# A pair's keys get their norm first, activation sums go one in two steps, and residual reloads wait for a split

## The chip, the cores and the metric

The kernel runs on one core of one Trainium2 chip. The metric is the device time of one execution in microseconds (us); less is better. The core has five engines with a queue of instructions each: TensorE (PE in the profile, its weight loads PEld) multiplies matrices, VectorE (DVE) and ScalarE (ACT) work elementwise, GpSimd (POOL) does some elementwise work and issues transfers, SyncE (SP) issues transfers. Each queue runs in its own order; semaphores hold an instruction until what it reads is there.

## The reference

One decoder layer on a sequence of 512 tokens, width 2048, in float32. Cut to what matters here:

```python
h = rms_norm(x, attn_norm)
proj = h @ w_in
qf, kf, vf, ff, qn, kc, vc, ks, vs, kw, vw, gt = split(proj)
qf = rms_norm(qf, fox_q_norm)          # 8 "fox" heads of 128
kf = rms_norm(kf, fox_k_norm)
s = einsum(qf, kf) * scale + cum[q] - cum[k]
o_fox = masked_softmax(s) @ vf
...
o_nsa = gate0 * o_c + gate1 * o_s + gate2 * o_w
x = x + concat(o_fox, o_nsa) @ w_out
h = rms_norm(x, ffn_norm)
x = x + (silu(h @ w_gate) * (h @ w_up)) @ w_down
```

`cum` is a running sum of log gates, so the fox heads have a bias for every pair of query and key. The other eight heads (compressed, selected and window branches, merged by gates) are computed earlier and are touched by the change only in passing.

## The kernel before

**Products.** Each float32 operand is split in a high and a low part of a shorter type. ACT writes the high part (`act(..., AF.Copy)`, L95), DVE the rest by a subtraction (`tt`, L92). A product is three matmuls, high by high, high by low and low by high (`mm3`, L259 to L261; L1057 and L1379 are the same in other loops). So each tile of weights passes SP (load), ACT (high part), DVE (low part) and PE, which may start a tile when the high part is there and needs the low part two matmuls later. `ws_*` are the loaded weights, `wp_*` their parts.

**Seven products for eight.** Most projections work by a scheme that replaces eight products of half matrices by seven, with sums of weights and sums of activations. The sums of activations are the "forms": `forms_45`, `forms_6` and `forms_3` make them on DVE (L976, L977, L984, L985, L994) and ACT (L991), a few instructions at each step, into `f4_u`, `f5_u`, `f6_u` for u from 0 to 7. They are first needed in the pair phase below.

**Stages.** The stretch that the change touches runs from about 390 to 840 us. First come the last single projections, `stagger(kf(1), qf(1), vf(2))`: the keys and queries of head 1 and the values of head 2. Beside them, woven in, run head 0's attention, and a generator `extra` with the forms: `among(main, extra, start, every)` takes a step of `extra` behind every so many steps of `main`. In this stage `extra` has 30 steps: five each of `forms_45` for u of 5, 6 and 7, and three each of `forms_6` for u of 0 to 4. What is left of it when `main` ends is run by `run(extra)`.

Then comes the pair phase. `seven` computes for a pair of outputs the seven products; `pair(h)` gives one head's keys and queries this way, `vpair(h)` the values of two heads. After its products a pair normalizes both outputs: their squares (`squares`), the sums over a head by a matmul with ones (`ss_k*`, L1104; `ss_q*`, L431), reciprocal square roots, and splits into parts. For the keys that gives `kf*`; for the query a split tile `qq`, and the four small instructions L443 to L446 on DVE that make `qs_q*`, the factors by which scores are scaled. This second part of `pair` runs beside the next pair's products.

Beside the products run the attentions of the heads 1 to 7 (`fox`, stepped by `attend`). `SPANS` gives for each head the ticks between which its 17 steps are spread; a tick is a step of the loop over pairs. A head multiplies scores in four blocks of query rows (`s_f*3` with 512 columns, then 384, 256 and 256), for which GpSimd makes bias tiles `nbf` from the factors (L847, L848); DVE adds the bias and finds the maxima (L602), ACT takes exponentials (L608) and scales (L617, `p_f`), PE transposes (`pT_f`, L633), and the transposed probabilities are multiplied by the values (`of`).

The output projection (from about 660 us) uses the seven products again. Its residual sums x1 are written to `x1d` in DRAM by GpSimd's queue (L1268). `form_again(pair)` reloads the tiles `pair` and `pair + 8` as `x1r` (L1285, GpSimd's queue as well, 256 KB each), from which the second half of the layer gets its raw forms. Its weights are loaded and split by `parts_apart`.

**Order.** In the attention stages a scheduler decides the order in each engine's queue, from dependencies and the order of the code; a step moved in the code moves rows on all engines. In the output projection and behind it the order is that of the code. `highs` is a list of instructions that wrote high parts; its last one serves as a time mark for transfers that shall not start earlier.

Of the kernel before, what the change touches and what calls it, by code (L numbers as in the profile page):

```python
# [9 lines left out]
F32 = mybir.dt.float32  # L10
# [7 lines left out]
P = 128  # L18
# [65 lines left out]
def hybrid_layer(ctx: ExitStack, tc: tile.TileContext, xT, vec, ffb, wfg, wfirst, win, cmpw, wout, wos, wgu, wdn, out):  # L84
# [123 lines left out]
    def split2(dst, src, scale=None):  # L208

        if scale is None:  # L210
            h = act(dst[0], src, AF.Copy)
            tt(dst[1], src, dst[0].bitcast(F32), op=OP.subtract)
        else:
            h = act(dst[0], src, AF.Copy, scale=scale)
            nc.vector.scalar_tensor_tensor(dst[1], src, scale, dst[0].bitcast(F32), op0=OP.mult, op1=OP.subtract)
        return h
# [153 lines left out]
    def gain(i):  # L370
        return gains[:, i:i + 1]
# [42 lines left out]
    def squares(name, z):  # L414

        sq = ftile(f"sq_{name}")
        sb = ap_.tile([P, T], F32, tag="sb", name=f"sb_{name}")
        nc.scalar.activation(sq[half], z[half], AF.Square)
        nc.scalar.activation(sb[half], z[second_half], AF.Square)
        nc.vector.tensor_tensor(sq[half], sq[half], sb[half], op=OP.add)  # L420
        return sq

    def square_sums(name, sq, tag, bufs=1):

        fr = ap_.tile([P, T], FR, tag="fr", name=f"fr_{name}")
        o = ps.tile([P, NB, 2], F32, tag=tag, name=f"ss_{name}", bufs=bufs)
        split2([fr[half], fr[second_half]], sq[half])
        if bufs > 1:
            yield
        for i in range(NB):  # L430
            nc.tensor.matmul(o[:, i], fr[:, i * P:(i + 1) * P], ones[:, :2], start=(i == 0), stop=(i == NB - 1), skip_group_check=True)  # L431
        return o
# [16 lines left out]
    def place():  # L449
        r = qq[:, turns[0] % 2]  # L450
        turns[0] += 1
        return [r[:, p] for p in range(2)]
# [630 lines left out]
    def pair(h):  # L1083

        k, q = [f"{m}f{h}" for m in "kq"]
        t, z = yield from seven(("p", h), (k, q))
        yield POST
        assert h - 2 in scored
        r = place()
        split2(r, z, gain(V_FQ))  # L1090
        sq = squares(q, z)
        yield
        oq = square_sums(q, sq, "t", 2)
        next(oq)
        yield
        sq = squares(k, t)
        yield
        oq = yield from oq
        fr = ap_.tile([P, T], FR, tag="fr", name=f"fr_{k}")
        split2([fr[half], fr[second_half]], sq[half])  # L1100
        yield
        yield
        ok = ps.tile([P, T], F32, tag="t", name=f"ss_{k}", bufs=2)
        nc.tensor.matmul(ok, ones, fr, start=True, stop=True)  # L1104
        yield
        live[q] = r, *factors(q, oq)
        y = ftile(f"y_{k}")
        rsqrt(y, ok, float(HD), ftile(f"tmp_{k}"), False)
        nc.vector.scalar_tensor_tensor(t, t, gain(V_FK), y, op0=OP.mult, op1=OP.mult)
        r = ap_.tile([P, KV], FR, tag="kv", name=k, bufs=5)[:, 64:64 + 2 * T].rearrange("p (s t) -> p s t", s=2)  # L1110
        first_keys[k] = r[:, :, :P]
        r = [r[:, p] for p in range(2)]
        split2(r, t)
        live[k] = r
        yield

    def vpair(h):
# [13 lines left out]
    def among(main, extra, start, every):  # L1131
        for i, _ in enumerate(main):
            yield
            if i >= start and (i - start) % every == 0:
                next(extra, None)
# [3 lines left out]
            next(steps, None)  # L1139
            yield  # L1140

    SPANS = {1: (0, 45), 2: (45, 73), 3: (73, 101), 4: (101, 157), 5: (157, 185), 6: (185, 213), 7: (213, 241)}
    STEPS = 17
    tick = [0]
    heads = {h: fox(h) for h in SPANS}
# [35 lines left out]
    live["x6"] = only.enter_context(tc.tile_pool(name="x6", bufs=1, side="right"))  # L1181
    paced[0] = 4
    extra = chain(*[forms_45(u, True) for u in range(5, HALF)], *[forms_6(u) for u in early6])
    weave(among(stagger(kf(1), qf(1), vf(2)), extra, 0, 1), fox(0), 4 * NK, FS, 18)
    run(extra)
    extra = chain(*[forms_3(u) for u in range(HALF)])
    assert nproj[0] == FIRST7
# [93 lines left out]
    def form_again(pair):  # L1281

        ts = [ftile(f"x1r_{n}") for n in (pair, pair + HALF)]
        for i, t in enumerate(ts):
            nc.gpsimd.dma_start(t, x1d[pair + HALF * i])  # L1285
        yield
        for i, t in enumerate(ts):
            raw_forms(pair + HALF * i, t)
        raw = live["raw"]
        form_sums(raw)  # L1290
        dst = forms[pair].rearrange("p s f t -> p s (f t)")
        src = raw[:, 0:7].rearrange("p f t -> p (f t)")
        if pair < 6:
            act(dst[:, 0], src, AF.Copy)
        yield
        if pair == 6:
            act(dst[:, 0], src, AF.Copy)
        tt(dst[:, 1], src, dst[:, 0].bitcast(F32), op=OP.subtract)
        yield
# [42 lines left out]
    def parts_apart(src, name, off):  # L1342
        st = ws_tile(f"{name}")
        load(st, src)
        wp = parts_tile(f"wp_{name}")
        wp = [cut(wp, at + off, HALF * P) for at in (0, HALF * P)]
        act(wp[0], st, AF.Copy)
        yield
        tt(wp[1], st, wp[0].bitcast(F32), op=OP.subtract)
        yield  # L1350
        return wp
# [693 lines left out]
```

## Time and profile before

| | |
|---|---|
| runs, median of 3 | 2089.14 us (2088.11 to 2091.69) |
| the profiled execution | 2089.46 us |
| its span | 2087.8 us |
| PE busy | 2063.7 us |
| DVE, ACT, POOL busy | 1803.2, 1070.4, 323.9 us |
| mean granted clock of PE | 0.998 of full speed |
| DMA packets | 424.22 MB |

The span runs from the first to the last instruction in the profile. A row of a timeline gives start, duration, engine, line, operation and the tiles with buffer numbers left out, and in brackets how long the engine idled before it and what released it. Durations of matmuls overlap, since they are pipelined: what one costs PE is the distance from its start to the next one's. PE's waits are few: the page's busy share is 99%.

### The profile page before, as it was taken

The numbers are of one execution on the slowest core, as the hardware profiler recorded it, in microseconds if no ns is written. First come the engines' busy times: TensorE is split into PE (matmuls) and PEld (weight loads), VectorE is DVE, ScalarE is ACT, GpSimd is POOL, SyncE is SP. The second block draws the span as 40 slices with busy tenths as digits, with TensorE's granted clock in tenths as the row PEclk, the third lists the DMA queues.
The fourth block names the chain that finished last, engine by engine and source line by source line (L and its number), as shares of the span: only waits on it lengthen the run. The fifth ranks groups of instructions, "written<-read, shape, count | busy, mean of one in ns | idle before, by whom it ended". The sixth has DMA issues, their size and how long they took to land.

```text
span 2087.8 us, 40036 instructions
## 1 busy us (share of the span) xinstructions
PE 2063.7 (99%) x16189; PEld 1976.5 (95%) x16189; DVE 1803.2 (86%) x2744; ACT 1070.4 (51%) x1408; POOL 323.9 (16%) x489
## 2 busy tenths in 40 slices
PE   9999999899999999999999999999999999999999
PEld 8888989799998988999999999999999999999999
DVE  6688779878777877999999999999999987889998
ACT  6555556457676555443343344433433455565554
POOL 1032232422121011111111111111111000000000
PEclk9999999999999999999999999999999999999999
DMA  5685776867775575676767777777777797579865
GB/s 211 208 183 164 178 173 180 196 172 209 219 187 187 189 238 184 169 209 185 194 191 189 203 183 184 210 182 198 188 190 203 241 327 258 155 237 329 298 177 149
DMA packets 142153, 424.22 MB, mean 203 GB/s; under 512 B 17608, under 2 KB 17608, under 8 KB 141968
## 3 DMA queue, kind: packets, MB, share of 16 engines
q1 hardware_dynamic: 91168, 289.21, 41.3%
q0 software_dynamic: 44176, 106.19, 26.6%
q10 hardware_dynamic: 6624, 26.27, 3.3%
q8 instruction: 126, 2.06, 0.4%
q14 instruction: 59, 0.48, 0.1%
HBM read 389.34 MB, written 124.53 MB: 246 GB/s over the span
## 4 chain that ended last, share of the span: by engine, by line
PE 87%; DVE 6%; ACT 4%; issue 2%; DMA 1%; POOL 0%; ACTq 0%; SPq 0%; POOLq 0%; DVEq 0%
PE q L1790 39%; PE pd L1929 13%; PE pd L1934 7%; PE ps_kf L1057 3%; PE ps_vs L540 2%; PE ps_vf L540 2%; PE po L261 2%; PE po L260 2%; PE po L259 2%; PE po L1379 1%; PE ps_qn L259 1%; PE ps_qn L261 1%; PE ps_qn L260 1%; PE ps_first L261 1%; PE ps_first L259 1%
## 5 line engine op out<-in xcount | busy, mean ns | idle before, releaser
L95 ACT ACTIVATE bigm<-r 128x1792 fp32r<-128x1792 f32 x174 | 298.3, 1714 | 462.6 <-PE q L1790 315.6
L92 DVE TENSOR_TENSOR bigm<-r,bigm 128x1792 fp32r<-128x1792 f32 x174 | 351.3, 2019 | 10.2 <-ACT bigm L95 9.7
L92 DVE TENSOR_TENSOR r<-r 128x512 f32<-128x512 f32 x522 | 267.1, 512 | 30.1 <-DMA r<-wgu 18.0
L141 POOL DMA_DIRECT2D wsum<-wdn x176 | 120.1, 689 | 702.2 <-ACT bigm L95 609.4
L1790 PE MATMUL q<-bigm 128*128 128x256 f32 x1848 | 217.5, 276 | 0.2
L1790 PE MATMUL q<-formy,bigm 128*128 128x256 f32 x1848 | 216.9, 276 | 0.0
L1790 PE MATMUL q<-forma,bigm 128*128 128x256 f32 x1848 | 216.8, 276 | 0.0
L1790 PE MATMUL q<-formx,bigm 128*128 128x256 f32 x1848 | 216.8, 276 | 0.0
L1790 PEld LDWEIGHTS q<-bigm 128*128 128x128 f32 x1848 | 213.3, 188 | 0.6 <-DVE bigm L92 0.3
L1790 PEld LDWEIGHTS q<-forma,bigm 128*128 128x128 f32 x1848 | 213.0, 188 | 0.1
L1790 PEld LDWEIGHTS q<-formy,bigm 128*128 128x128 f32 x1848 | 213.0, 188 | 0.1
L1790 PEld LDWEIGHTS q<-formx,bigm 128*128 128x128 f32 x1848 | 212.9, 188 | 0.0
L1929 PE MATMUL pd<-bigm 128*128 128x256 f32 x1200 | 146.9, 276 | 0.0
L1929 PEld LDWEIGHTS pd<-bigm 128*128 128x128 f32 x1200 | 141.0, 188 | 0.0
L92 DVE TENSOR_TENSOR bigm<-wd,bigm 128x1024 fp32r<-128x1024 f32 (+1 forms) x62 | 107.7, 1738 | 13.3 <-ACT bigm L95 13.0
L95 ACT ACTIVATE bigm<-rawm 128x768 fp32r<-128x768 f32 (+2 forms) x72 | 66.0, 927 | 96.8 <-PE pd L1934 62.2
L95 ACT ACTIVATE bigm<-wd 128x1024 fp32r<-128x1024 f32 (+1 forms) x62 | 91.1, 1469 | 12.1 <-DVE wd L92 6.1
L92 DVE TENSOR_TENSOR bigm<-rawm,bigm 128x768 fp32r<-128x768 f32 (+2 forms) x72 | 75.5, 1057 | 23.1 <-ACT bigm L95 22.3
L1934 PE MATMUL pd<-bigm 128*128 128x256 f32 x600 | 80.7, 276 | 0.0
L141 POOL DMA_DIRECT2D fsump<-win x72 | 48.5, 742 | 203.3 <-ACT wp_qn L95 46.8
L1057 PE MATMUL ps_kf<-bigm,wp_kf 128*128 128x256 f32 x576 | 77.0, 282 | 1.0 <-ACT wp_kf L95 0.9
L1057 PEld LDWEIGHTS ps_kf<-bigm,wp_kf 128*128 128x128 f32 x576 | 71.6, 188 | 3.0 <-ACT wp_kf L95 1.8
(592 smaller groups left out, 4342.0 us busy)
## 6 DMA issues: line engine op xcount, KB each, us to landing
r<-wgu SPq DMA_DIRECT2D x174, 512.0 KB, 4.4
wsum<-wdn POOLq DMA_DIRECT2D x176, 256.0 KB, 5.0
rawm<-ad SPq DMA_DIRECT2D x44, 512.0 KB, 6.8
wd<-wdn SPq DMA_DIRECT2D x40, 512.0 KB, 6.0
wd<-wsum SPq DMA_DIRECT2D x40, 512.0 KB, 7.1
ad<-cb ACTq DMA_DIRECT2D x22, 896.0 KB, 6.5
fsump<-win POOLq DMA_DIRECT2D x72, 256.0 KB, 6.2
rawm<-ad SPq DMA_DIRECT2D x44, 384.0 KB, 3.6
```

Source lines behind the costliest of these rows:

```text
L92: return pin(nc.vector.tensor_tensor(*args, op=op))
L95: return pin(nc.scalar.activation(*args, **kw))
L141: d = nc.gpsimd.dma_start(step[0], step[1], **step[2])
L259: nc.tensor.matmul(o, lh, rh, start=start, stop=False)
L260: nc.tensor.matmul(o, lh, rl, start=False, stop=False)
L261: nc.tensor.matmul(o, ll, rh, start=False, stop=stop)
L540: nc.tensor.matmul(z[2 * b + t][:, :cols[n]], x[:, xp, at], wp[n][kk], start=(c == 0 and kk == 0 and n == 0 and (t == 0 or gcols is not No ...
L1057: nc.tensor.matmul(z, w[wp][:, u * P:(u + 1) * P], form(f, u)[xp], start=(fresh and m == 0), stop=(m == len(todo) - 1), skip_group_check=True)
L1379: nc.tensor.matmul(q[b][:, h * 256:(h + 1) * 256], w[wp][:, u * P:(u + 1) * P], a[xp], start=(h == 0 and u == 0 and wp == 0 and xp == 0), ...
L1790: nc.tensor.matmul(o, w[wp][:, fb, cs], a[:, xp, fa], start=(k == 0 and h == 0 and wp == 0 and xp == 0), stop=(g == NG - 1 and kk == 1 and ...
L1929: nc.tensor.matmul(b[q][k][:, h * 256:(h + 1) * 256], w[0][:, fb, q * P:(q + 1) * P], a[xp][:, fa], start=(j == 0 and h == 0 and xp == 0), ...
L1934: nc.tensor.matmul(b[q][k][:, h * 256:(h + 1) * 256], w[1][:, fb, q * P:(q + 1) * P], a[0][:, fa], start=False, stop=(j == NJ - 1), skip_g ...
```

## The change

Three parts, none of which adds or removes arithmetic.

`pair`: the keys' squares and their sum come ahead of the query's split and squares; both sums are followed by the keys' scaling and splits, and the query's factors are made last. Keys and factors are handed on in the same step as before. `SPANS`: the spans of heads 1 to 7 begin and end two ticks later (head 7 ends one later).

`among(..., extra, 0, 2)`: beside the keys and queries of head 1 a step of the activation sums is taken at every second step of the projections instead of at each.

`form_again`: the reloads of pairs above 0 depend on the last high split of weights issued so far, which `parts_apart` now puts into `highs`.

```diff
--- before.py
+++ after.py
@@ -1086,24 +1086,20 @@
         t, z = yield from seven(("p", h), (k, q))
         yield POST
         assert h - 2 in scored
-        r = place()
-        split2(r, z, gain(V_FQ))
+        sq = squares(k, t)
+        yield
+        fr = ap_.tile([P, T], FR, tag="fr", name=f"fr_{k}")
+        split2([fr[half], fr[second_half]], sq[half])
+        qr = place()
+        split2(qr, z, gain(V_FQ))
+        yield
         sq = squares(q, z)
         yield
+        ok = ps.tile([P, T], F32, tag="t", name=f"ss_{k}", bufs=2)
+        nc.tensor.matmul(ok, ones, fr, start=True, stop=True)
         oq = square_sums(q, sq, "t", 2)
         next(oq)
         yield
-        sq = squares(k, t)
-        yield
-        oq = yield from oq
-        fr = ap_.tile([P, T], FR, tag="fr", name=f"fr_{k}")
-        split2([fr[half], fr[second_half]], sq[half])
-        yield
-        yield
-        ok = ps.tile([P, T], F32, tag="t", name=f"ss_{k}", bufs=2)
-        nc.tensor.matmul(ok, ones, fr, start=True, stop=True)
-        yield
-        live[q] = r, *factors(q, oq)
         y = ftile(f"y_{k}")
         rsqrt(y, ok, float(HD), ftile(f"tmp_{k}"), False)
         nc.vector.scalar_tensor_tensor(t, t, gain(V_FK), y, op0=OP.mult, op1=OP.mult)
@@ -1111,7 +1107,11 @@
         first_keys[k] = r[:, :, :P]
         r = [r[:, p] for p in range(2)]
         split2(r, t)
+        yield
+        oq = yield from oq
+        yield
         live[k] = r
+        live[q] = qr, *factors(q, oq)
         yield
 
     def vpair(h):
@@ -1139,7 +1139,7 @@
             next(steps, None)
             yield
 
-    SPANS = {1: (0, 45), 2: (45, 73), 3: (73, 101), 4: (101, 157), 5: (157, 185), 6: (185, 213), 7: (213, 241)}
+    SPANS = {1: (0, 47), 2: (47, 75), 3: (75, 103), 4: (103, 159), 5: (159, 187), 6: (187, 215), 7: (215, 242)}
     STEPS = 17
     tick = [0]
     heads = {h: fox(h) for h in SPANS}
@@ -1181,7 +1181,7 @@
     live["x6"] = only.enter_context(tc.tile_pool(name="x6", bufs=1, side="right"))
     paced[0] = 4
     extra = chain(*[forms_45(u, True) for u in range(5, HALF)], *[forms_6(u) for u in early6])
-    weave(among(stagger(kf(1), qf(1), vf(2)), extra, 0, 1), fox(0), 4 * NK, FS, 18)
+    weave(among(stagger(kf(1), qf(1), vf(2)), extra, 0, 2), fox(0), 4 * NK, FS, 18)
     run(extra)
     extra = chain(*[forms_3(u) for u in range(HALF)])
     assert nproj[0] == FIRST7
@@ -1282,7 +1282,9 @@
 
         ts = [ftile(f"x1r_{n}") for n in (pair, pair + HALF)]
         for i, t in enumerate(ts):
-            nc.gpsimd.dma_start(t, x1d[pair + HALF * i])
+            d = nc.gpsimd.dma_start(t, x1d[pair + HALF * i])
+            if pair:
+                tc.add_manual_dep(d.ins, highs[-1].ins.name, PACE)
         yield
         for i, t in enumerate(ts):
             raw_forms(pair + HALF * i, t)
@@ -1344,7 +1346,7 @@
         load(st, src)
         wp = parts_tile(f"wp_{name}")
         wp = [cut(wp, at + off, HALF * P) for at in (0, HALF * P)]
-        act(wp[0], st, AF.Copy)
+        highs.append(act(wp[0], st, AF.Copy))
         yield
         tt(wp[1], st, wp[0].bitcast(F32), op=OP.subtract)
         yield
```

In the first place the queue is DVE's, at the first half of the weights of head 1's queries (`wp_qf1_0`). The rows ahead of it before the change; `d4`, `d5`, `f5` and `f6` with `acc` are activation sums, `t_kf1`, `sb_kf1` and `sq_kf1` the keys of head 1:

```order
L396 TENSOR_TENSOR t_kf1_4393<-ps_kf1_4258,rstd_181 128x512
L984 TENSOR_TENSOR acc_180<-d4_7_4359,bigm_79 128x256
L994 TENSOR_TENSOR f5_7_4376<-d4_7_4359,f5_7_4376 128x256
L985 TENSOR_TENSOR acc_180<-acc_180,bigm_79 128x256
L472 TENSOR_TENSOR sb_kf1_4396<-t_kf1_4393 64x512
L994 TENSOR_TENSOR f6_7_4377<-acc_180,f6_7_4377 128x256
L473 TENSOR_TENSOR sq_kf1_4395<-sq_kf1_4395,sb_kf1_4396 64x512
L92 TENSOR_TENSOR wp_qf1_0_4403<-ws_qf1_0_4401,wp_qf1_0_4403 128x1024
```

The rows ahead of the same split in the changed kernel (`qs_qf0` are the query factors of head 0):

```order
L443 TENSOR_TENSOR qs_qf0_4334<-qs_qf0_4334 128x4
L984 TENSOR_TENSOR d4_6_4343<-d4_6_4343,bigm_79 128x256
L994 TENSOR_TENSOR f6_5_4298<-acc_180,f6_5_4298 128x256
L444 TENSOR_SCALAR qs_qf0_4334<-qs_qf0_4334 128x4
L985 TENSOR_TENSOR d4_6_4343<-d4_6_4343,bigm_79 128x256
L445 TENSOR_TENSOR qs_qf0_4334<-qs_qf0_4334 128x4
L92 TENSOR_TENSOR wp_qf1_0_4375<-ws_qf1_0_4373,wp_qf1_0_4375 128x1024
```

Before, the split stood behind the whole sums of u = 5, 6 and 7 and behind the squares of head 1's keys; now it stands in the middle of those of u = 6, and the keys' rows come after it.

In the second place the queue is PE's, in the pair phase, at the scores of head 3 (`s_f33` is the block of 512 columns, `s_f30` the last one; L1057 are the products of pairs that fill the time between). Before:

```order
L260 MATMUL s_f33_5779<-kf3_5760,qq_228 128x512
L261 MATMUL s_f33_5779<-kf3_5760,qq_228 128x512
L260 MATMUL s_f32_5808<-kf3_5760,qq_228 128x384
L261 MATMUL s_f32_5808<-kf3_5760,qq_228 128x384
L1057 MATMUL ps_kf424_5736<-f6_7_4377,wp_kf4_6_5860 128x256
L1057 MATMUL ps_vf400_5906<-bigm_79,wp_vf4_0_5900 128x256 x4
L259 MATMUL s_f31_5825<-kf3_5760,qq_228 128x256
L260 MATMUL s_f31_5825<-kf3_5760,qq_228 128x256
L261 MATMUL s_f31_5825<-kf3_5760,qq_228 128x256
L1057 MATMUL ps_vf400_5906<-bigm_79,wp_vf4_0_5900 128x256 x2
L598 MATMUL s_f30_5849<-kf3_5760,qq_228 128x256
L599 MATMUL s_f30_5849<-kf3_5760,qq_228 128x128
```

In the changed kernel:

```order
L1057 MATMUL ps_kf411_5582<-bigm_79,wp_kf4_5_5784 128x256 x6
L259 MATMUL s_f33_5797<-kf3_5703,qq_228 128x512
L260 MATMUL s_f33_5797<-kf3_5703,qq_228 128x512
L261 MATMUL s_f33_5797<-kf3_5703,qq_228 128x512
L1057 MATMUL ps_kf411_5582<-bigm_79,wp_kf4_5_5784 128x256 x12
L259 MATMUL s_f32_5820<-kf3_5703,qq_228 128x384
L260 MATMUL s_f32_5820<-kf3_5703,qq_228 128x384
L261 MATMUL s_f32_5820<-kf3_5703,qq_228 128x384
L1057 MATMUL ps_kf411_5582<-bigm_79,wp_kf4_5_5784 128x256 x6
L259 MATMUL s_f31_5838<-kf3_5703,qq_228 128x256
L260 MATMUL s_f31_5838<-kf3_5703,qq_228 128x256
L261 MATMUL s_f31_5838<-kf3_5703,qq_228 128x256
```

The blocks of scores came one right behind the other; now products of the pair stand between them. Behind the last block stood 42 products ahead of the transposes `pT_f30`, now 48 (before, 18 of them of `wp_vf4_0` and 24 behind; now 12 of `wp_kf4_6`, 24 of `wp_vf4_0` and 12 of `wp_vf4_1`).

In the third place the queue is GpSimd's, in the output projection: stores of x1 (L1268) and the reloads (L1285), with - for before and + for the changed kernel:

```order
 L1285 DMA x1r_0_8739<-x1d0_7201 128x512
 L1285 DMA x1r_8_8740<-x1d8_7209 128x512
+L1268 DMA x1d4_7205<-c7_40_8571 128x512
+L1268 DMA x1d12_7213<-c7_41_8572 128x512
 L1285 DMA x1r_1_8792<-x1d1_7202 128x512
 L1285 DMA x1r_9_8793<-x1d9_7210 128x512
-L1268 DMA x1d4_7205<-c7_40_8571 128x512
-L1268 DMA x1d12_7213<-c7_41_8572 128x512
+L1268 DMA x1d5_7206<-x1_5_8791 128x512
 L1285 DMA x1r_2_8871<-x1d2_7203 128x512
-L1268 DMA x1d5_7206<-x1_5_8791 128x512
 L1285 DMA x1r_10_8872<-x1d10_7211 128x512
```

The reload of pair 1 (tiles 1 and 9) has changed places with the stores of tiles 4 and 12, and that of pair 2 comes behind the store of tile 5.

## The prediction

> **What bounds the kernel now.** I read the page first, then the waits of TensorE (PE), then its timeline and windows at the longest wait.
>
> ```profile
> span 2087.8 us, 40036 instructions
> PE 2063.7 (99%) x16189; PEld 1976.5 (95%) x16189; DVE 1803.2 (86%) x2744; ACT 1070.4 (51%) x1408; POOL 323.9 (16%) x489
> ...
> 850.00:2050.00 1200.00, 1200.00 (x10579) 1199.93 (x10578) 1104.63 (x1377) 552.50 (x461) 130.86 (x193) 1.00 0.75 213
> ```
>
> PE is busy for 2063.7 of 2087.8 us: 24.1 us idle. In the window from 850 to 2050 us (columns: length, busy us of PE, weight load, DVE, ACT, POOL, then granted clock, DMA share, GB/s) it is never idle, and the change moves nothing there. So at most the 24.1 us can go, plus time in which PE is busy at a low clock. The groups of waits say where the idle time lies:
>
> ```profile
> PE ps_qf L261 <- DVE wp_qf L92: 6.1, 1, 6.1
> PE pT_f L633 <- ACT p_f L617: 4.1, 4, 1.0
> PE po L1379 <- ACT wp_o L95: 1.7, 2, 1.1
> ```
>
> Three edits, three rows (total us, times, longest). I price each where its wait stands.
>
> **Step of the activation sums (every second step).** The longest wait is one gap at 397 us:
>
> ```profile
> 396.99 0.33 PE L261 MATMUL s_f<-kf,qq 128*128 128x384 f32 x1
> 403.45 0.80 PE L261 MATMUL ps_qf<-bigm,wp_qf 128*128 128x512 f32 x1 [6.13 <-DVE wp_qf L92]
> 404.04 0.63 PE L259 MATMUL ps_qf<-bigm,wp_qf 128*128 128x512 f32 x1
> 404.47 0.63 PE L260 MATMUL ps_qf<-bigm,wp_qf 128*128 128x512 f32 x1
> ...
> 407.87 0.39 PE L259 MATMUL ps_qf<-bigm,wp_qf 128*128 128x512 f32 x1
> 408.10 0.40 PE L260 MATMUL ps_qf<-bigm,wp_qf 128*128 128x512 f32 x1
> ```
>
> A 384-wide matmul keeps PE for 0.175 us (starts 396.64, 396.82, 396.99 in the same timeline), so the next should start at 397.17: 403.45 - 397.17 = 6.28 us lost. Then matmuls start 0.43 us apart (404.04 to 404.47) instead of 0.23 (407.87 to 408.10): eleven starts in 407.87 - 403.45 = 4.42 us, ten pitches (ten x 0.2275 = 2.27), so 2.15 more. Together **8.4 us**. The windows give the reason for the second part:
>
> ```profile
> 396.00:408.00 12.00, 5.87 (x18) 4.48 (x17) 11.91 (x26) 4.69 (x11) 8.63 (x9) 0.72 0.70 201
> ...
> 402.00:404.00 2.00, 0.55 (x1) 0.50 (x2) 2.00 (x4) 0.63 (x1) 1.13 (x2) 0.50 0.46 134
> ...
> 408.00:410.00 2.00, 2.00 (x11) 1.64 (x10) 1.97 (x4) 0.20 (x1) 0.72 (x2) 1.00 0.99 391
> ```
>
> The granted clock is 0.50 after the long idle time and 1.00 again from 408 on. The Trainium skill, "TensorE: Matmul & The Clock Gate", Part 1: The HAM clock gate, says that the array falls to half its clock after an idle window of about 3.4 us and needs about as much busy time to recover; the trace agrees, with 0.50 from 402 to 404. By that rule a wait shorter than about 3.4 us that remains there keeps the full clock, and the sum below stands as it is.
>
> In the same windows DVE is full (11.91 of 12 us), so the gap is DVE's order:
>
> ```profile
> 387.09 1.28 DVE L976 TENSOR_TENSOR d<-bigm 128x512 f32<-128x512 f32 x2
> 388.29 0.74 DVE L977 TENSOR_TENSOR d<-d 128x256 f32<-128x256 f32 x2
> ...
> 402.19 1.21 DVE L92 TENSOR_TENSOR wp_qf<-ws_qf,wp_qf 128x1024 fp32r<-128x1024 f32 x1
> ```
>
> Between the sums' first row at 387.09 and the low half of the query's weights at 402.19 stand 38 instructions before and 18 after, in the order of after: three 512 wide (0.60 apart), eleven 256 wide (0.34), four tiny (0.07) = 1.80 + 3.74 + 0.28 = 5.8 us. The split would start at 392.9 and end 1.14 later, at 394.1; PE asks for it near 396. Both parts of the loss go, 8.4 us. What is late next: twelve sums now stand ahead of later splits. The next split that PE waits for is that of the second quarter of the values' weights, at 419.58:
>
> ```profile
> 398.89 0.88 DVE L994 TENSOR_TENSOR f<-d,f 128x256 fp32r<-128x256 f32 x1
> ...
> 419.58 1.23 DVE L92 TENSOR_TENSOR wp_vf<-ws_vf,wp_vf 128x1024 fp32r<-128x1024 f32 x1
> ...
> 425.19 0.16 DVE L439 TENSOR_TENSOR qs_qf<-ss_qf,eps_col 128x4 f32<-128x4 f32 x1 [2.40 <-PE ss_qf L431]
> ```
>
> Counted by pitches from 387.09, as above, the old order reaches it at 415.9, so 3.65 us were idle time and lengthened rows (the one at 398.89 is 0.88 long, its like 0.41). The new order reaches it at 412.5 (three sums' nine rows have gone behind it, small rows ahead): ready at 413.6, and up to 3.65 later. PE, from 389.18 on by its own pitches, asks at 413.6. The new wait is 0 to 3.65; the middle is 1.85, and the transposes a few rows on wait some 0.6 for ACT's L617: I take 2.5. The sums moved later fall into DVE's idle time (2.40 us ahead of 425.19). Net **-5.9** (bounds -8.4 if the new wait vanishes, -2 if DVE stays the bound).
>
> **Keys' norm first, spans two steps later.** Four heads (2, 3, 5 and 6) show one pattern; here is head 2:
>
> ```profile
> 489.56 0.50 PE L260 MATMUL s_f<-kf,qq 128*128 128x512 f32 x1
> ...
> 492.07 0.23 PE L599 MATMUL s_f<-kf,qq 128*128 128x128 f32 x1
> 492.13 2.38 PE L1057 MATMUL ps_kf<-bigm,wp_kf 128*128 128x256 f32 x19
> 494.35 2.88 PE L1057 MATMUL ps_kf<-f,wp_kf 128*128 128x256 f32 x24
> 498.26 1.09 PE L633 MATMUL pT_f<-ident,p_f 128*128 128x128 f32 x8 [1.03 <-ACT p_f L617]
> 499.73 0.96 PE L1057 MATMUL ps_kf<-bigm,wp_kf 128*128 128x256 f32 x6 [0.38 <-ACT wp_kf L95]
> ...
> 496.30 1.91 ACT L617 ACTIVATE p_f<-p_f,st_f 128x512 f32<-128x512 f32 x4
> ```
>
> After the last score, 43 matmuls at 0.113 us (4.86 us) are all that covers the softmax, which needs some 6.05: 1.19 lost at the transposes, and 0.54 at 499.73, since ACT's split of the next weights is queued behind L617: 1.73 a head, 6.9 in four. Small waits ahead of the scores (up to 0.24 each, at 489.56 for one) add some 0.55: 2.3 a head, 9.2 in all. In the new order 48 matmuls (5.42 us) stand there for heads 3, 5 and 6 and 60 (6.78) for head 2; the scores are drawn apart (the third follows the second after 1.93 instead of 0.4 us). Ahead of the scores it is the keys' chain that counts:
>
> ```profile
> 479.60 0.39 PE L1104 MATMUL ss_kf<-fr_kf,ones 128*128 128x512 f32 x1
> ...
> 488.82 0.69 DVE L92 TENSOR_TENSOR kf<-t_kf,kf 128x512 fp32r<-128x512 f32 x1
> ```
>
> From the keys' sum (479.60) to their low half DVE and ACT took 9.2 us, and PE has 8.0 us of other work there in both orders. In the new order the query's squares no longer run ahead of the keys' on ACT and DVE, so I expect 8.3. Left per head: 0.3 (keys' low half), 0.15 (scores), 0.5 (transposes) and 0.3 (ACT's split) = 1.2 to 1.3, some 1.6 in head 2, 5.2 in all. Gain 4.0; heads 1, 4 and 7, which wait for little now, may give 0.5 back: **-3.5** (bounds -7, nearly all gone, and +1, waits only moved). The edit adds no instruction; the query's four tiny factors (L443 to L446) come last instead of first.
>
> **Reloads behind the splits.** GpSimd issues four reloads while PE works on the first output tiles:
>
> ```profile
> 743.50 1.08 POOL L1285 DMA_DIRECT2D x1r<-x1d  x2 [0.17 <-issue]
> ...
> 740.00:745.00 5.00, 5.00 (x47) 5.00 (x46) 3.47 (x5) 2.65 (x3) 3.26 (x6) 1.00 0.97 335
> ...
> x1r<-x1d POOLq DMA_DIRECT2D x4, 256.0 KB, 8.1
> ...
> ws_o<-wos SPq DMA_DIRECT2D x1, 512.0 KB, 8.4
> ...
> 751.04 1.06 ACT L95 ACTIVATE wp_o<-ws_o 128x1024 fp32r<-128x1024 f32 x1 [3.86 <-PE po L1379]
> ...
> 752.15 4.83 PE L1379 MATMUL po<-osums_a,wp_o 128*128 128x256 f32 x40 [1.14 <-ACT wp_o L95]
> ```
>
> The weights that ACT splits at 751.04 were landing for 8.4 us (the row from wos), while the DMA was 97% busy at 335 GB/s with four reloads of 256 KB. PE waited 1.14 for it. The change sends the pair of 743.50 (512 KB) behind the next pair's stores: 512 KB at 350 GB/s = 1.46 us earlier for the weights. The later reloads are covered by PE work of 24 x 0.2275 = 5.5 us a tile; queued behind the waiting issue on POOL are only stores and the next reloads. **-1.4** (bounds -1.8 and 0, if the queue is not in order of issue).
>
> Sum: -5.9 - 3.5 - 1.4 = -10.8. The profiled execution took 2089.46 us (its span and 1.7 us around it), 0.3 above the median of the runs: 2078.7 from it, 2078.3 from the median; I say **2078.5**.
>
> **Rivals.** (A) *Only the gap goes*: ACT's chain behind the scores is as long as before, so the waits of the pair phase move by a few rows and stay. For: L617 alone is 1.91 us and comes last in both orders. Against: 5 to 17 more matmuls cover it. 2089.5 - 5.9 - 1.4 = 2082.2. (B) *The gap moves with DVE's work*: the new wait takes its upper bound of 3.65, is long enough for the granted clock to fall again, which costs the same 2.15, and 0.6 follow: part two saves 8.4 - 6.4 = 2.0, the others 3.5 / 2 and 1.4: 2089.5 - 2.0 - 1.75 - 1.4 = 2084.4. Against: it needs all of the old delay in the new order, and PE's waits give ACT and DVE time to catch up. (C) *All waits go*: -8.4 - 7 - 1.8 = 2072.3. (D) **Slower**: the query's factors, now behind the keys' low half on DVE, hold back GpSimd's bias tiles, which the scores' two PSUM banks wait for:
>
> ```profile
> L847 POOL TENSOR_SCALAR nbf<-ckb,ncq,qs_qf x32: 444/714/2989, 398.4 to 650.0; 128x512 f32<-128x512 f32 x8, 128x384 f32<-128x384 f32 x8, 128x256 f32<-128x256 f32 x8, 128x128 f32<-128x128 f32 x8
> ...
> 640.65 3.27 POOL L847 TENSOR_SCALAR nbf<-ckb,ncq,qs_qf 128x512 f32<-128x512 f32 x2 [17.78 <-DVE qs_qf L446]
> 643.88 1.96 POOL L848 TENSOR_SCALAR_AFFINE_SELECT nbf<-nbf 128x128 f32<-128x128 f32 x2
> ```
>
> A bias usually takes 0.71 (the median) and 0.29 us, but there 1.63 and 0.98. In the new order the third score, which needs the first one's bank, comes three matmuls of 512, twelve and six of 256 and three of 384 columns behind it: 0.68 + 2.04 + 0.53 = 3.25 us. The factors' end (0.5 estimated after the score), bias and mask 2.6 and DVE's read of 0.67 are 3.8, so 0.55 late; with the next bias as slow, and the longest of 2.99 in it, some 2.5 a head, in six heads 15: 2089.5 - 7.3 + 15 = 2097.2. It decides from 2.0 a head on; with the median durations (0.5 + 1.0 + 0.67) it is 1.1 us early. The Trainium skill, "SBUF — State Buffer", Who interferes with whom, speaks against the change here: a DVE instruction with two SBUF inputs and a GpSimd instruction that reads SBUF block each other for a whole instruction, so that a bias beside one of DVE's splits would take up to a split (1.14) longer. The trace agrees, with biases of 444 to 2989 ns; by the rule alone, with every bias hit, the time would be that of this rival. (E) *The change doesn't do what it says*: the gap moves as in B, and the pairs' waits stay as in A: 2089.5 - 2.0 - 1.4 = 2086.1, no difference. Against: two unlikely cases at once.
>
> **How the numbers follow.** Forecast 0.50, A 0.22, B 0.08, C 0.11, D 0.03, E 0.06. Range 2072.0 to 2085.0: from C to B, with a few tenths each; outside are D, E and the ends of B and C. The bound of 0.2% (4.2 us, about what a measurement of this kernel can tell from no change) is 2085.0 and 2093.3: faster 0.90, same 0.07, slower 0.03.
>
> **What would show it.** Right: no wait for wp_qf near 397 and a granted clock of 1.00 there; one of 1 to 3 us for wp_vf or p_f near 405 to 415; pT_f waits under 0.8 each; no wait of po at 752. Wrong: a granted clock of 0.50 between 400 and 420; pT_f waits of 1 us in four heads (A); PE waiting for s_f on DVE's L602 with POOL rows above 1.5 us (D).

## The result and the profile after

| | before | changed | ratio, 95% interval |
|---|---|---|---|
| first runs (4 each), median | 2089.78 us | 2078.11 us | 0.9942 [0.9925, 0.9960] |
| second runs (5 of the changed kernel) | 2088.92 us | 2077.58 us | 0.9944 [0.9931, 0.9958] |
| span of the profiled execution | 2087.8 us | 2076.6 us | |

The kernel is 11.3 to 11.7 us faster, clear of noise and inside the range that was forecast. First the page of the changed kernel and its groups of waits of PE (total us, times, longest):

```profile
span 2076.6 us, 40008 instructions
...
PE 2058.7 (99%) x16189; PEld 1974.0 (95%) x16189; DVE 1802.1 (87%) x2744; ACT 1070.6 (52%) x1408; POOL 322.5 (16%) x489
...
PE s_f L259 <- DVE st_f L602: 2.5, 3, 1.0
...
PE po L259 <- DVE t_vf L1070: 1.0, 1, 1.0
...
PE ss_kf L478 <- DVE fr_kf L92: 0.8, 1, 0.8
...
PE po L261 <- DVE wp_o L92: 0.5, 1, 0.5
```

Of the three rows of before (6.1 for wp_qf, 4.1 for the transposes pT_f behind L617, 1.7 for wp_o) none is left on top. Smaller ones have come: scores wait for DVE's L602, which frees their bank; the first product of the output projection waits for DVE's L1070, which the prediction didn't have; the sum of head 1's keys waits for its split; and the output projection waits for a low half on DVE. PE's busy time fell by 5.0 us as well, 2.15 of it the matmuls at half clock; where the rest comes from is open.

Since most instructions are the same in both kernels, the starts of the same matmuls on PE divide the time into stages. "Lead" runs to the first product of head 1's queries, "projections" from there to the first product of the pair phase (L1057), "pairs" to the first product of the output projection, "closing" to its first seven-product step, "output" to the first product of the feed-forward part, "rest" to the last matmul. Between the two kernels one matmul leaves the projections and four pass from the closing to the pairs; the other stages hold the same ones (us):

| kernel | lead | projections | pairs | closing | output | rest |
|---|---|---|---|---|---|---|
| before | 394.37 | 47.99 | 201.70 | 52.20 | 126.20 | 1259.50 |
| changed | 395.33 | 40.39 | 197.12 | 52.72 | 125.45 | 1259.79 |
| difference | +0.96 | -7.60 | -4.58 | +0.52 | -0.75 | +0.29 |

The lead has the same instructions in both; it varied between 393.17 and 396.34 in the thirteen profiles of this study, most of it in one early wait (zkT for zks, 0.4 to 2.3 us). So a single profile's total says little below 2 us, and stages are compared below. "Rest" stays within 0.7 us. The new wait in the closing is that for L1070: 0.97 to 1.18 us in each kernel with the new order and the new spans, 0.32 with the new order alone (e4), none in the others.

The place of the gap, in the changed kernel's timelines (PE, then DVE) and windows:

```profile
396.46 0.39 PE L259 MATMUL ps_qf<-bigm,wp_qf 128*128 128x512 f32 x1
396.69 0.39 PE L260 MATMUL ps_qf<-bigm,wp_qf 128*128 128x512 f32 x1
396.91 0.39 PE L261 MATMUL ps_qf<-bigm,wp_qf 128*128 128x512 f32 x1
...
404.44 0.47 PE L478 MATMUL ss_kf<-fr_kf,ones 128*128 128x512 f32 x1 [0.77 <-DVE fr_kf L92]
```

```profile
394.45 1.22 DVE L92 TENSOR_TENSOR wp_qf<-ws_qf,wp_qf 128x1024 fp32r<-128x1024 f32 x1
...
403.35 0.94 DVE L92 TENSOR_TENSOR fr_kf<-sq_kf,fr_kf 64x512 fp32r<-64x512 f32 x1
...
415.11 1.19 DVE L92 TENSOR_TENSOR wp_vf<-ws_vf,wp_vf 128x1024 fp32r<-128x1024 f32 x1
```

```profile
396.00:398.00 2.00, 2.00 (x10) 1.68 (x9) 1.97 (x6) 1.34 (x2) 2.00 (x2) 1.00 1.00 332
...
404.00:406.00 2.00, 1.56 (x8) 1.41 (x9) 1.97 (x6) 2.00 (x5) 1.05 (x3) 1.00 0.85 165
```

The low half of the query weights is done at 395.6, where DVE's next row starts, 1.3 us ahead of the matmul that needs it (396.91), and the granted clock stays at 1.00. What is late next is not the split of the values' weights (415.11), for which PE doesn't wait, but the small split of head 1's keys at 403.35: 0.93 us between 403.51, when its matmul could start, and 404.44.

### The profile page after: what moved, and what is told of

It is laid out like the page before. It is cut to its first block, busy times and chain, and to the rows that moved or that the text cites. A ratio compares the mean times of both kernels' runs of the same rounds, so it can differ in the third digit from the quotient of the medians.

```text
span 2076.6 us, 40008 instructions
## 1 busy us (share of the span) xinstructions
PE 2058.7 (99%) x16189; PEld 1974.0 (95%) x16189; DVE 1802.1 (87%) x2744; ACT 1070.6 (52%) x1408; POOL 322.5 (16%) x489
## 4 chain that ended last, share of the span: by engine, by line
PE 82%; issue 8%; DVE 6%; ACT 2%; POOL 2%; DMA 1%; POOLq 0%; ACTq 0%; SPq 0%; DVEq 0%
PE q L1792 40%; PE pd L1931 13%; PE pd L1936 7%; PE ps_vs L540 2%; PE po L1381 2%; PE ps_vf L540 2%; PE ps_qn L259 1%; PE ps_qn L261 1%; PE ps_qn L260 1%; PE ps_first L261 1%; POOL osum L141 1%; PE ps_first L259 1%; PE po L261 1%; PE po L259 1%; PE po L260 1%
## 5 line engine op out<-in xcount | busy, mean ns | idle before, releaser
L1931 PEld LDWEIGHTS pd<-bigm 128*128 128x128 f32 x1200 | 141.0, 188 | 0.0
L1057 PE MATMUL ps_kf<-bigm,wp_kf 128*128 128x256 f32 x576 | 76.1, 281 | 0.7 <-ACT wp_kf L95 0.4
L1936 PEld LDWEIGHTS pd<-bigm 128*128 128x128 f32 x600 | 74.3, 188 | 0.0
```

The source lines that it names most:

```text
L1057: nc.tensor.matmul(z, w[wp][:, u * P:(u + 1) * P], form(f, u)[xp], start=(fresh and m == 0), stop=(m == len(todo) - 1), skip_group_check=True)
L1931: nc.tensor.matmul(b[q][k][:, h * 256:(h + 1) * 256], w[0][:, fb, q * P:(q + 1) * P], a[xp][:, fa], start=(j == 0 and h == 0 and xp == 0), ...
L1936: nc.tensor.matmul(b[q][k][:, h * 256:(h + 1) * 256], w[1][:, fb, q * P:(q + 1) * P], a[0][:, fa], start=False, stop=(j == NJ - 1), skip_g ...
```

## The experiments

Each kernel was timed against the kernel before on the same chip. All numbers in the stage columns are from its profile. That of f3 is its slowest execution (2086.17 us; its five lie between 2079.43 and 2086.17), so its stages add up to more than its median. The intervals of e2, e4 and f2 come near 1 or touch it, so for these the stages are the evidence.

| run | median us | ratio, 95% interval | projections | pairs | output |
|---|---|---|---|---|---|
| e1: sums at every second step alone | 2080.13 | 0.9958 [0.9945, 0.9970] | 40.37 | 201.27 | 125.98 |
| e2: pairs' order and spans | 2085.97 | 0.9988 [0.9979, 0.9997] | 48.62 | 198.10 | 124.67 |
| e3: reloads' dependency alone | 2090.07 | 1.0004 [0.9995, 1.0013] | 48.08 | 201.57 | 125.07 |
| e4: pairs' order alone | 2086.93 | 0.9990 [0.9981, 0.9999] | 47.39 | 199.76 | 125.32 |
| f1: e1 and e2 together | 2076.67 | 0.9944 [0.9932, 0.9957] | 40.47 | 196.99 | 124.68 |
| f2: spans alone | 2086.85 | 0.9990 [0.9981, 1.0000] | 48.14 | 198.87 | 124.61 |
| f3: changed, spans three later | 2080.88 | 0.9968 [0.9956, 0.9981] | 40.48 | 200.50 | 128.71 |
| f4: sums start five steps later | 2081.44 | 0.9967 [0.9955, 0.9979] | 43.70 | 200.88 | 126.02 |
| h1: f1 with masks in order | 2075.92 | 0.9936 [0.9924, 0.9949] | 40.48 | 196.54 | 125.12 |
| h2: f1, sums at every third step | 2078.68 | 0.9952 [0.9939, 0.9964] | 40.19 | 199.58 | 125.47 |
| h3: the changed kernel again | 2077.58 | 0.9944 [0.9931, 0.9958] | 40.48 | 196.99 | 125.76 |

### Each part alone

**e1**, the step of the activation sums:

```diff
-    weave(among(stagger(kf(1), qf(1), vf(2)), extra, 0, 1), fox(0), 4 * NK, FS, 18)
+    weave(among(stagger(kf(1), qf(1), vf(2)), extra, 0, 2), fox(0), 4 * NK, FS, 18)
```

> Before, with the activation sums stepped at every second step alone. Theory (the three parts add up, each in its own stage): PE is 7.6 us earlier at the first product of the pair phase, as in the changed kernel (443.49 - 395.50 = 47.99 us between the first query product of head 1 and it before, 40.39 after), the four transposes' waits of 1.0 us and the wait of 1.1 us for wp_o stay, and the time is 2089.8 - 7.6 = 2082.2 (2081 to 2083). Rival (DVE owes the moved sums, and the time comes back in the pair phase): the pair phase starts 7 us earlier but ends less than 5 us earlier; 2085 or more.

The projections shrink by 7.62 us, as in the changed kernel, and nothing is given back later (pairs -0.43). The time is 0.9 us below the expected range; the rival falls. This one number carries some three quarters of the result (8.6 of some 11.5 us).

**e2**, the order in `pair` with the new `SPANS` (both as in the change, nothing else).

> Before, with the new order in the pairs and the later spans alone. Theory: the gap of 6.1 us at 397 us and its low clock stay; the pair phase is shorter by 4.6 us and the next stage longer by 0.5 (201.70 to 197.13 and 52.19 to 52.71 in the two profiles): 2089.8 - 4.1 = 2085.7 (2084.5 to 2086.7). The new wait of scores for DVE's L602 (2.5 us in three heads) is there without the other parts. Rival (the pair phase gains only because DVE comes into it with other work behind it): under 2 us, 2088 or more.

The pair phase is 3.60 us shorter, the closing 0.64 longer, and the wait for L602 is there (2.5 us in three heads) without the other parts. The time fell by 2.7 where 4.1 was expected, inside the range that was given. Next to e1 the pairs gain 4.28 (201.27 to 196.99 in f1), 0.7 more: the parts nearly add up.

**e3**, the dependency alone.

> Before, with the reloads' dependency alone. Theory: the wait of po for wp_o of 1.14 us at 752 us goes, a wait of some 0.5 us comes 40 us later, net -0.8: 2089.0 (2088.4 to 2089.4), within what the measurement can tell from no change; the rows tell it. Rival (the wait goes for another reason, since the weights arrive 10 us earlier in the program): the wait for wp_o of about 1 us stays; 2089.8.

No gain in time (1.0004). The stage shows what was expected, 1.13 us less, with the wait at 752 us gone and one of 0.30 in its place, at 812 us.

**e4**, the order in `pair` with the old `SPANS`.

> Before, with the new order in the pairs, but the old spans. Theory (the two need each other: with the keys first, the query's factors come last and the scores must move later): in this order PE has 2.7 to 3.2 us between the query's sums and the first score of heads 2, 3, 5 and 6, where the changed kernel has 4.1 to 4.6; so PE waits for L602 in more heads and longer, 1 to 2 us each, some 6 in all, against 6.9 saved at the transposes: 2088.5 (2087 to 2091). Rival (the order in the pairs alone carries the gain): 2086 or less.

The pair phase gains 1.94. The trade is the expected one, seen in the groups of waits of this kernel:

```profile
PE s_f L259 <- DVE st_f L602: 4.8, 5, 1.1
PE pT_f L633 <- ACT p_f L617: 1.1, 2, 0.8
```

Of the 4.1 us at the transposes 3.0 go, and with them the smaller waits around them; 4.8 us come at the scores, in five heads (2.5 in three heads in the changed kernel). The order alone carries part of the gain, not all; 2086.93 lies just outside the theory's range and doesn't reach the rival's.

### Two parts together, and what the dependency is worth

**f1** is the changed kernel without the dependency:

```diff
-            d = nc.gpsimd.dma_start(t, x1d[pair + HALF * i])
-            if pair:
-                tc.add_manual_dep(d.ins, highs[-1].ins.name, PACE)
+            nc.gpsimd.dma_start(t, x1d[pair + HALF * i])
```

> The changed kernel without the reloads' dependency (parts one and two together). Theory (the dependency is worth little, since in the kernels with part one or part two alone the weights from wos landed in 7.4 and 6.7 us instead of 8.4 and PE lost 0.37 and nothing there, though all four reloads were issued beside them): within 1 us of the changed kernel, 2078 to 2079; PE's loss at the seven products 0 to 0.7 us, and the wait of 0.6 us of po for the low half at 790 us does not come. Rival (the prediction's term of 1.4 us): 2079.5 or more, with the wait of about 1.1 us for wp_o back.

It is as fast as the changed kernel: 2076.67 against 2078.11 and 2077.58, with ratios that can't be told apart, and below the range that was expected. PE doesn't wait for the high half of the weights from wos, though all four reloads are issued beside them. And the later reload shows what the dependency costs. First the changed kernel (GpSimd, ACT, DVE, PE), then f1 (ACT, DVE):

```profile
785.28 1.10 POOL L1285 DMA_DIRECT2D x1r<-x1d  x2 [2.40 <-ACT wp_o L95]
...
786.70 0.72 ACT L95 ACTIVATE raw<-x1r,vt 128x512 f32<-128x512 f32 x1 [1.10 <-DMA x1r<-x1d]
...
787.46 1.61 DVE L92 TENSOR_TENSOR raw<-raw 128x512 f32<-128x512 f32 x3 [2.17 <-ACT raw L95]
788.99 1.22 DVE L92 TENSOR_TENSOR wp_o<-ws_o,wp_o 128x1024 fp32r<-128x1024 f32 x1
...
790.26 0.50 PE L261 MATMUL po<-bigm,wp_o 128*128 128x512 f32 x1 [0.48 <-DVE wp_o L92]
```

```profile
783.71 1.32 ACT L95 ACTIVATE raw<-x1r,vt 128x512 f32<-128x512 f32 x2
...
785.06 1.61 DVE L92 TENSOR_TENSOR raw<-raw 128x512 f32<-128x512 f32 x3 [1.18 <-ACT raw L95]
786.59 1.22 DVE L92 TENSOR_TENSOR wp_o<-ws_o,wp_o 128x1024 fp32r<-128x1024 f32 x1
```

With the dependency GpSimd holds the reload for 2.40 us, ACT then waits for it to land, DVE waits for ACT, and behind DVE's three rows stands the low half that PE needs. Without it ACT has both tiles at once, and PE doesn't wait for the low half. The stage "output" is 125.45, 125.76, 125.07 and 128.71 us in the four kernels with the dependency and 124.61 to 126.20 in the nine without: no gain. The rows of all thirteen profiles tell why. Counted by starts, PE loses 0.3 to 1.9 us (0.9 on average; 1.9 in before) beside the four reloads in the nine without the dependency, and at most 0.3 in the four with it: the load behind the one from wos takes 6.5 to 8.1 us in the nine and 4.6 to 5.9 in the four. At the late reloads it loses nothing in the nine, and 0.5 (e3), 1.2 (the changed kernel), 1.4 (h3) and 4.5 us (f3, half clock included) in the four. So the dependency does what it was meant to do, and the gain is lost again later. The wait of 1.14 us for wp_o in the profile of before was the largest of its kind: f4 has one of 0.65, the other seven without the dependency none above 0.1.

**h3** is the changed kernel again, on the chip of h1 and h2.

> The changed kernel as it is, beside the two others. Theory (the reloads' dependency wins the wait at the seven products and pays with one of 0.3 to 3 us for wp_o's low half behind late reloads): the wait of po for DVE's wp_o near 790 us is there again, and the time is 0.5 to 2 us above that of the changed kernel without the dependency (2076.7): 2077.2 to 2078.7. Rival (the dependency gains 1.4 us as predicted): 2075.5 or less.

The wait for DVE's wp_o is there again (0.80 us at 789.68), and 2077.58 lies in the theory's range and not the rival's. The times of f1 and h3 differ by less than their intervals, so this rests on the rows.

### Spans, and what made the keys late

**f2** has the new `SPANS` line alone.

> Before, with the later spans alone. Theory (the keys' low half decides when scores can run, and the spans only place them): in this order heads 3 and 6 have 4.6 us between the keys' sum and their first score, against 7.8 before, where the low half needs 9.2, so PE waits there 3 to 4 us each, while their transposes' waits (1.7 each) go; heads 2 and 5 keep theirs: 2088.7 + 7 - 3.5 = 2092 (2090 to 2095). Rival (spans two steps later are what draws the scores apart and ends the transposes' waits): 2086 or less.

The theory falls: 2086.85, and the pair phase is 2.83 us shorter; the rival's 2086 isn't reached either. Heads 2 and 5 keep their transposes' waits (1.02 and 1.03 us), and what goes lies in heads 3 and 6. Here is head 3 in the kernel before (PE, DVE) and in f2 (PE, DVE):

```profile
507.35 0.39 PE L1104 MATMUL ss_kf<-fr_kf,ones 128*128 128x512 f32 x1
...
516.75 0.69 DVE L92 TENSOR_TENSOR kf<-t_kf,kf 128x512 fp32r<-128x512 f32 x1
```

```profile
506.67 0.40 PE L1104 MATMUL ss_kf<-fr_kf,ones 128*128 128x512 f32 x1
...
513.20 0.50 PE L260 MATMUL s_f<-kf,qq 128*128 128x512 f32 x1 [0.26 <-DVE kf L92]
...
512.46 0.68 DVE L92 TENSOR_TENSOR kf<-t_kf,kf 128x512 fp32r<-128x512 f32 x1
```

From the keys' sum to their low half it took 9.4 us before and 5.8 in f2, with the same instructions in the chain. The 9.2 us on which the prediction's step rested were not the length of a chain: before, three splits of weights stood on DVE between the two (at 509.99, 513.03 and 515.61), in f2 one (at 511.25). That the scheduler orders them by where the scores stand is a reading of these rows. The wait is 0.26 us, and 0.45 for L602 behind it, not 3 to 4.

**f3** moves the spans one step further.

```diff
-    SPANS = {1: (0, 47), 2: (47, 75), 3: (75, 103), 4: (103, 159), 5: (159, 187), 6: (187, 215), 7: (215, 242)}
+    SPANS = {1: (0, 48), 2: (48, 76), 3: (76, 104), 4: (104, 160), 5: (160, 188), 6: (188, 216), 7: (216, 242)}
```

> The changed kernel with the spans one more step later (0 to 48, 48 to 76, 76 to 104, 104 to 160, 160 to 188, 188 to 216, 216 to 242). Theory (the wait of scores for L602 that is left, 0.95, 0.92 and 1.12 us in heads 2, 5 and 7, comes from factors that are made some 0.7 us too late): there are 0.7 to 1.2 us more between the query's sums and the scores of these heads, and the three waits fall under 0.3 each: 2078.1 - 2 = 2076 (2075 to 2077.5). Rival (GpSimd's bias tiles are as late as the factors are, since DVE's splits hold them back): the waits stay, 2078.

Wrong as well: the scores' waits fell in heads 2 and 5 only (to 0.64 and 0.46) and rose to 1.58 in head 7, and the transposes wait again, 1.24 to 1.69 us in four heads; the pairs take 3.38 us more. The median, 2080.88, is above the rival's 2078 too. The rival's mechanism shows in GpSimd's rows of head 2 (then DVE and PE):

```profile
482.74 0.82 POOL L141 DMA_DIRECT2D osum<-wos  x1 [0.49 <-issue]
483.34 2.32 POOL L847 TENSOR_SCALAR nbf<-ckb,ncq,qs_qf 128x256 f32<-128x256 f32 x2
485.59 0.56 POOL L848 TENSOR_SCALAR_AFFINE_SELECT nbf<-nbf 128x128 f32<-128x128 f32 x2
...
483.64 1.21 DVE L92 TENSOR_TENSOR wp_kf<-ws_pair,wp_kf 128x1024 fp32r<-128x1024 f32 x1
...
485.94 0.48 DVE L602 CUSTOM_DVE_ANT_0 p_f<-s_f,nbf,qs_qf 128x256 f32<-128x256 f32 x1 [1.09 <-POOL nbf L848]
...
492.17 1.09 PE L633 MATMUL pT_f<-ident,p_f 128*128 128x128 f32 x8 [1.09 <-ACT p_f L617]
```

Two bias tiles that take 0.56 and 0.45 us in the changed kernel take 2.32 together, behind a transfer's issue and beside DVE's split of 1.21, so the softmax ends later. The Trainium skill, "SBUF — State Buffer", Who interferes with whom, says that a DVE instruction with two SBUF inputs and a GpSimd instruction that reads SBUF exclude each other; this row agrees, with 2.32 us beside a split of 1.21, but no run here parts it from the transfer's issue.

**h1** makes GpSimd mask a bias tile before it makes the next one.

```diff
-            nc.gpsimd.tensor_scalar(nb[:, :n], ck[:, :n], ncq[:, i, h:h + 1], q[2][:, i:i + 1] if len(q) == 3 else 1.0, op0=OP.add, op1=OP.mult)
-            nc.gpsimd.affine_select(nb[:, n - P:n], ...
+            d = nc.gpsimd.tensor_scalar(nb[:, :n], ck[:, :n], ncq[:, i, h:h + 1], q[2][:, i:i + 1] if len(q) == 3 else 1.0, op0=OP.add, op1=OP.mult)
+            if masks:
+                tc.add_manual_dep(d.ins, masks[-1].ins.name, PACE)
+            m = nc.gpsimd.affine_select(nb[:, n - P:n], ...
...
+            masks.append(m)
```

> Parts one and two of the change (no reload dependency), with each bias tile of GpSimd masked (L848) before the next one is made (L847); before, the two first tiles were made and then masked, so that DVE's first L602 waited for both. Theory (the wait of scores left in heads 2, 5 and 7, 0.85 to 1.21 us each, is GpSimd's: the factors are there 2 us before the first L602, and the second bias stands between): the first L602 comes 0.6 to 0.8 us earlier in each head and the three waits fall under 0.4: 2076.7 - 2 = 2074.7 (2074 to 2075.7). Rival (the later bias becomes as late as the first was early, since DVE's splits hold GpSimd back): waits move to the next score or to the transposes, 2076.5.

In the changed kernel (first) DVE's first L602 of head 2 waits until both tiles are made and masked; in h1 (second, where L850 is the mask of L848) it starts behind the first mask:

```profile
478.88 1.68 POOL L847 TENSOR_SCALAR nbf<-ckb,ncq,qs_qf 128x512 f32<-128x512 f32 x2
480.52 0.54 POOL L848 TENSOR_SCALAR_AFFINE_SELECT nbf<-nbf 128x128 f32<-128x128 f32 x2
...
480.85 0.75 DVE L602 CUSTOM_DVE_ANT_0 p_f<-s_f,nbf,qs_qf 128x512 f32<-128x512 f32 x1 [1.58 <-POOL nbf L848]
...
481.66 0.39 PE L259 MATMUL s_f<-kf,qq 128*128 128x256 f32 x1 [0.79 <-DVE st_f L602]
```

```profile
478.40 1.05 POOL L847 TENSOR_SCALAR nbf<-ckb,ncq,qs_qf 128x512 f32<-128x512 f32 x1
479.53 0.29 POOL L850 TENSOR_SCALAR_AFFINE_SELECT nbf<-nbf 128x128 f32<-128x128 f32 x1
...
479.86 0.75 DVE L602 CUSTOM_DVE_ANT_0 p_f<-s_f,nbf,qs_qf 128x512 f32<-128x512 f32 x1 [1.07 <-POOL nbf L850]
```

So the wait is GpSimd's, as the theory says, but only part of it goes: the three losses fall from 0.85, 0.95 and 1.21 (f1) to 0.44, 0.64 and 0.69, some return at the transposes, and the stage gains 0.45 us, a quarter of what was expected. The median, 2075.92, is the lowest of all kernels, 0.75 us below f1's, which the intervals don't resolve.

### The gap and the clock

**f4** keeps a step of the sums at each step, but starts five later.

```diff
-    weave(among(stagger(kf(1), qf(1), vf(2)), extra, 0, 1), fox(0), 4 * NK, FS, 18)
+    weave(among(stagger(kf(1), qf(1), vf(2)), extra, 5, 1), fox(0), 4 * NK, FS, 18)
```

> Before, with the activation sums at every step as before, but started five steps later. Counted by DVE's pitches, the low half of the first query weights is ready at 397.4 plus the 1.4 that rows were longer there, some 1.6 us after PE asks, and that of the second half 2 to 3 us after PE asks: two shorter waits in place of one of 6.1. Theory (the single long idle time costs twice, 6.28 as idle time and 2.15 as half clock): the granted clock stays at 1.00 from 396 to 412, the loss there is 3.5 to 5 us, time 2084 to 2086. Rival (half the clock follows from the sum of idle time): clock 0.5 to 0.75 in some window there, 2086.5 or more.

Its timeline of PE and two of its windows:

```profile
396.85 0.50 PE L261 MATMUL ps_qf<-bigm,wp_qf 128*128 128x512 f32 x1 [0.72 <-DVE wp_qf L92]
...
404.68 0.50 PE L261 MATMUL ps_qf<-bigm,wp_qf 128*128 128x512 f32 x1 [1.00 <-DVE wp_qf L92]
...
396.00:398.00 2.00, 1.27 (x6) 0.97 (x6) 1.94 (x3) 0.39 (x1) 2.00 (x3) 1.00 0.37 139
...
404.00:406.00 2.00, 1.32 (x5) 0.86 (x5) 1.94 (x4) 0.42 (x1) 1.93 (x2) 1.00 0.57 116
```

DVE is as full as before, yet the one wait of 6.1 has become two of 0.72 and 1.00, with a third of 0.43 at 414.25 for head 1's keys, and the granted clock stays at 1.00. The projections take 43.70 us, 4.3 less than before and 3.3 more than in the changed kernel. The sums are the same and come at the same rate, so it is where they stand against the splits that counts. The waits are shorter than the pitches gave (some 1.6 and 2 to 3), and 2081.44 is below the range of the theory. As a test of the rival, that the sum of idle time sets the clock, it is weak, since that sum fell as well.

**h2** takes the sums at every third step (`extra, 0, 3`).

> Parts one and two of the change, with a step of the activation sums at every third step instead of every second. Theory (the wait of 0.93 us at the keys' sum ss_kf of head 1 comes from the sums ahead of its split on DVE): by DVE's pitches that split is ready 2.4 us earlier (399.4 for 401.8), the wait goes, and the sums left over run into DVE's idle time: 2076.7 - 0.9 = 2075.8 (2075 to 2076.5). Rival (the sums left over are late for the pair phase, whose first products need them): PE waits for f or wp_kf behind 435 us, 2077.5 or more.

The rival has it. The wait at the keys' sum goes, but the projections are only 0.28 us shorter, and the pair phase is 2.6 us longer, with the left-over sums standing on DVE beside its first splits. By the stages every second step is the best of the three that were tried; the times of f1 and h2 overlap in their intervals.

## Why the prediction came out right

The forecast was 2078.5, the result 2078.1, but the terms are less exact than the sum: gap -7.6 for -5.9, pairs with closing -4.1 for -3.5, reloads -0.75 in the profile (nothing by the runs, whose times don't resolve it) for -1.4, and +1.25 from stages that the change leaves alone (lead and rest). Errors of either sign cancel, so that the total came within 1 us of the forecast is in part luck.

- **The gap.** "Both parts of the loss go, 8.4 us" is shown by e1 and by the clock rows, though the part of 2.15 us is a matter of where the low clock falls (last section); the split came at 394.45 to 395.6 where 392.9 to 394.1 was counted, in a run whose lead is 1 us longer. The new wait was sized too large and put in the wrong place: 2.5 for the values' split and the transposes, where there was 0.93 for a split of 64x512 that the count of rows had passed over as no weight split. The upper bound of 3.65 took DVE's old idle time and lengthened rows as if they had to come again; they didn't.
- **The pairs.** The size is right (-4.58 and +0.52 for -3.5), the picture only in part. The four transposes' waits for L617 went wholly, where 0.5 each was left in the sum. What was left came at the scores: rival D's mechanism, factors behind the keys' low half and bias tiles late on GpSimd, at 0.85 to 1.2 us in three heads, about half of the 2.0 a head that would have decided it. The 8.3 us expected from the keys' sum to their low half came out (7.6 to 8.6 in the six heads of the changed kernel, where before it was 9.1 to 10.6), but it is no fixed need: in f2 heads 3 and 6 take 5.8, in the old order. By the pair phase the order in `pair` and `SPANS` each gain 2 to 3 us alone (e4, f2), 3.6 together (e2). The wait for L1070 in the closing isn't in the sum.
- **The reloads.** The step that failed is "the later reloads are covered by PE work of 24 x 0.2275 = 5.5 us a tile". They are not: on DVE the low half of the weights stands behind the rows that need the reload. The sharing of DMA time is there, worth 0.9 us on average where 1.4 was counted (512 KB, 524288 bytes, at 350 GB/s are 1.50 us, not 1.46), and the loss at the late reloads takes it back. The term should have been near 0 with a bound on either side.
- **The rivals.** A (transposes' waits stay) is refuted by the changed kernel's groups of waits, B (the clock falls again) by its windows, and E falls with both. C (all waits go) fails by the 2.5 us left at the scores. Nothing was slower. The sign "one of 1 to 3 us for wp_vf or p_f near 405 to 415" didn't come; the 0.93 us lost at the keys' sum stand there instead.

## What to carry to other kernels

Where one engine bounds the time and another is full beside it for a while, look at which of the full engine's rows the bound one needs next; spreading the others cost nothing here at every second step (and 2.6 us of the pair phase at every third), and one long wait can cost more than its length: behind that of 6.1 us the matmuls ran at half clock for 2.15 us more. A delay measured between two instructions in a scheduled kernel is no chain's length until each row between them is shown to wait for the one before; here 9.4 us shrank to 5.8 without an edit to the chain. A wait for a transfer has another size in each profile, as its landing time has (6.0 to 8.4 us for the weights from wos without the dependency): look at the same transfer in other runs, and at what the transfers sent behind will hold up, before paying for it with a dependency.

## What the runs showed of the hardware that was not expected

The granted clock fell behind a shorter idle time than the prediction counted on. In f3 PE idles for 2.83 us at the late reload (PE's rows, then windows):

```profile
797.44 0.79 PE L261 MATMUL po<-bigm,wp_o 128*128 128x512 f32 x1 [2.83 <-DVE wp_o L92]
798.03 0.63 PE L259 MATMUL po<-bigm,wp_o 128*128 128x512 f32 x1
798.46 0.63 PE L260 MATMUL po<-bigm,wp_o 128*128 128x512 f32 x1
...
796.00:798.00 2.00, 0.56 (x1) 0.50 (x2) 1.99 (x3) 1.65 (x2) 0.00 (x0) 0.74 0.00 0
798.00:800.00 2.00, 2.00 (x6) 1.58 (x5) 0.98 (x1) 2.00 (x4) 0.55 (x1) 0.50 0.81 225
```

It is 0.50 from 798 to 800, and matmuls start 0.43 us apart until 800.17: six starts in 2.73 us where 1.37 would do, 1.4 us on top of the 2.99 lost before. The Trainium skill, "TensorE: Matmul & The Clock Gate", Part 1: The HAM clock gate, gives an idle window of about 3.4 us; here 2.83 was enough, and two waits of 0.72 and 1.00 in f4 were not. An early wait narrows this, that of zkT in the lead, in f3 (first two rows) and h1:

```profile
104.18 0.36 PE L734 MATMUL zkT<-ident,zks 64*128 64x64 f32 x1 [2.17 <-DVE zks L731]
...
104.00:106.00 2.00, 1.82 (x6) 0.73 (x7) 0.63 (x3) 0.58 (x2) 0.00 (x0) 0.51 1.02 396
```

```profile
104.27 0.28 PE L734 MATMUL zkT<-ident,zks 64*128 64x64 f32 x1 [1.58 <-DVE zks L731]
...
104.00:106.00 2.00, 1.74 (x11) 1.12 (x12) 0.71 (x3) 0.58 (x2) 0.00 (x0) 1.00 1.02 405
```

An idle time of 2.17 us lowered the clock, one of 1.58 didn't; each is one case. Nor does the fall come at a fixed point. In f3 it comes 2.0 and 2.4 us into the two idle times, and the clock is low for 3.41 us each time. In the five profiles that keep the gap (before, e2, e3, e4, f2) the idle time is 6.1 us in all, but the fall comes 3.7, 5.1, 3.9, 2.4 and 4.0 us into it, and the clock is low for 6.83 us, twice 3.41, in each. The later it falls, the more of the low time PE spends working: the matmuls behind the gap take 2.15 us more in before, 2.75 in e2 and 1.54 in e4. That difference of 1.21 us is the spread of "projections" between e2 (48.62) and e4 (47.39), and no effect of their edits.
